# A decoder trunk in which GLA and HGRN2 make and turn their carried keys later, and score products are tied into runs

## The chip, the cores and the metric

The kernel runs on one core of one Trainium2 chip, as one program. The metric is the device time of one execution, in microseconds. The core has a matmul engine (TensorE, PE in the rows), a vector engine (VectorE, DVE), an activation engine (ScalarE, ACT), a general engine (GpSimd, POOL) and a queue engine (SyncE, SP). Each takes its own instructions strictly in the order in which they stand in its queue, and waits on semaphores for the others.

## What is computed

One layer over a sequence of 1024 tokens of width 1024. A normalised and modulated input u is multiplied by one wide matrix; four causal token mixers (RWKV-7, GLA, mLSTM, HGRN2) work on slices of the product, each result is gated, projected, merged and added to the input. GLA and HGRN2 are one recurrence, with 4 heads each:

```python
def _chunk_gla(q, k, v, log_g, chunk):
    # S_t = diag(exp(log_g_t)) S_{t-1} + k_t v_t^T,  o_t = S_t^T q_t
    def step(state, blk):
        qc, kc, vc, gc = blk
        b = jnp.cumsum(gc, axis=2)
        rel = jnp.where(causal[:, :, None], b[:, :, :, None, :] - b[:, :, None, :, :], -jnp.inf)
        attn = jnp.einsum('bhik,bhjk,bhijk->bhij', qc, kc, jnp.exp(rel))
        o = attn @ vc + jnp.einsum('bhik,bhkv->bhiv', qc * jnp.exp(b), state)
        b_last = b[:, :, -1]
        state = (state * jnp.exp(b_last)[..., None]
                 + jnp.einsum('bhjk,bhjv->bhkv', kc * jnp.exp(b_last[:, :, None] - b), vc))
        return state, o
...
p = u @ w_in[l]
y_b = _gla(gq, gk, gv, g_code, gla_gk_up[l], gla_gk_b[l], gla_norm_g[l])
y_d = _hgrn2(hq, hf, hi, lower_bounds[l], hg_norm_g[l])
```

## The kernel before

The kernel has three stages. The first makes u and runs RWKV-7. The second runs eight units in the order HGRN2 head 0, GLA pair 0, HGRN2 1, mLSTM pair 0, HGRN2 2, GLA pair 1, HGRN2 3, mLSTM pair 1 (a GLA unit is two heads on the two halves of the partitions). The third merges and projects. This text is on the second, and there on `d_quarter` (HGRN2, 16 calls) and `b_quarter` (GLA, 8 calls).

A **unit** is worked in four quarters of 256 tokens, each of two chunks of 128. Behind each quarter `units` issues a part of the next unit's projections: `project` loads a weight block of 128 columns (`wraw`, one buffer, L297), ScalarE casts it to `whi` (L303), VectorE makes the rest `wlo` (L304), and `mm3` (L314 to L316) multiplies both with u in products of 128x512, 24 for a half of the tokens. These are the long products in TensorE's queue between which all else stands. Once a unit a column of another matrix (`gw`) goes through the same single buffer `wraw` and is summed by VectorE into `gacc` (L278, L280).

A **quarter** does this. Running sums of the log decay are made over 128, 64 and 32 tokens (`cums`, L828). The values are turned (`turn`: two transposes by TensorE, L921, and a ScalarE copy out of PSUM, L926). `carried` (L831) makes the keys decayed to the chunk's end, `kt` (ScalarE L837, VectorE L840), and turns them to `kT`; the products of kT with V (L982 in HGRN2, L1125 in GLA) are what the state gains. `qe` is the query decayed from the chunk's start. The causal block of a chunk is split into seven levels of pairs of blocks of s = 64, 32, 16, 8, 4, 2, 1 tokens (`LV`). For each, `level_factor` makes the decay factors (exponents on ScalarE, for s of 16 and less a difference on VectorE before), VectorE multiplies in q and k (L975, L977; L1136, L1139), and a score product follows: 26 small ones of 64x64 a quarter in HGRN2 (L994), 14 of 128x128 in GLA (L1148, seven per chunk, and a short one for the diagonal, L1150). VectorE copies them under masks into the score matrix (`ATd` L1008, `ATb` L1156), and TensorE multiplies that with V (L1012, L1165) and qe with the state (L1013, L1161). The output is normalised and, later, turned (L889).

**The order** is made by the compiler's scheduler: on each engine the ready instruction that stands first in the program goes first, by estimated times. Two helpers bind it: `together` raises the priority of a list of products and lets all others of the list stand behind the first (`issue_after` says that what is issued in its block on that engine stands behind the given instruction). Before the change HGRN2's score products go through `together`; GLA's are issued freely, and stand where their factors come ready.

## Time and profile before

| | |
|---|---|
| median of 3 runs | 1797.45 us (1797.1 to 1800.5) |
| the profiled execution | 1800.29 us, its span 1798.1 us |
| TensorE busy | 1710.5 us, 95% of the span |
| VectorE, ScalarE, GpSimd busy | 1161.5, 753.7, 325.9 us |
| mean granted TensorE clock | 0.981 |
| share of the chain that ended last | TensorE 72%, VectorE 13%, ScalarE 5%, DMA 3% |

The profile is of one execution. A row of the timeline gives the start, the duration, the engine, the line, the operation, the tile written <- the tiles read, the form, how many records it holds, and in brackets how long the engine sat idle before it and what ended that. Matmuls are pipelined, so that the distance from one start to the next tells what one costs, not the duration. A product with a full f32 operand stands as two records, a transpose and the long products as one.

### The profile page before, as it was taken

How to read it: one execution, taken by the hardware profiler on the slowest of the kernel's cores; microseconds unless marked ns; L12 is line 12 of the kernel's file. 1: busy time of each engine (PE TensorE's matmuls, PEld its weight loads, DVE VectorE, ACT ScalarE, POOL GpSimd, SP SyncE). 2: the span in 40 equal slices, each digit the busy share in tenths (PEclk: the TensorE clock that was granted, in tenths of full speed). 3: DMA queues.
4: the chain of work that ended last, by engine and by line, in shares of the span. 5: the costliest groups of instructions: out<-in, count | busy, mean ns of one | idle time of the engine just before them, and what ended most of it. 6: DMA issues, size and time to landing. Idle time of an engine off the chain costs nothing.

```text
span 1798.1 us, 28703 instructions
## 1 busy us (share of the span) xinstructions
PE 1710.5 (95%) x10515; PEld 1363.1 (76%) x10515; DVE 1161.5 (65%) x3173; ACT 753.7 (42%) x1780; POOL 325.9 (18%) x555
## 2 busy tenths in 40 slices
PE   5989999999999999999899999999889999989998
PEld 4766777877777778787678877887668888767786
DVE  7657868668667744766777546666887653565632
ACT  5633333333343336546534463547444342222221
POOL 4621112011111120000010001000010020276410
PEclk7989999999999999999999999999999999999999
DMA  9222222222221222121121212111111135666422
GB/s 298 58 73 45 55 74 66 50 71 56 59 77 47 71 55 59 48 65 39 56 59 51 68 47 66 60 54 39 56 48 57 54 97 187 200 215 200 136 89 76
DMA packets 224278, 147.30 MB, mean 82 GB/s; under 512 B 60511, under 2 KB 203018, under 8 KB 224138
## 3 DMA queue, kind: packets, MB, share of 16 engines
q1 hardware_dynamic: 208800, 109.23, 22.3%
q10 hardware_dynamic: 15338, 36.24, 5.6%
q8 instruction: 83, 1.36, 0.3%
q14 instruction: 57, 0.47, 0.1%
HBM read 111.88 MB, written 33.56 MB: 81 GB/s over the span
## 4 chain that ended last, share of the span: by engine, by line
PE 72%; DVE 13%; ACT 5%; DMA 3%; POOL 3%; issue 3%; SPq 0%; POOLq 0%; ACTq 0%; DVEq 0%
PE pj L314 15%; PE pj L316 15%; PE pj L315 14%; PE yw L732 3%; PE sc L683 3%; DMA wraw<-in_w_in_dram 2%; PE iv L315 2%; PE iv L316 2%; PE iv L314 2%; DVE adacc L229 1%; PE sc L994 1%; DVE tm L670 1%; PE sc L1148 1%; PE sc L620 1%; PE iv L921 1%
## 5 line engine op out<-in xcount | busy, mean ns | idle before, releaser
L314 PE MATMUL pj<-uh,whi 128*128 128x512 f32 x1344 | 548.8, 408 | 4.1 <-DVE rn L534 3.7
L316 PE MATMUL pj<-uh,wlo 128*128 128x512 f32 x1344 | 541.5, 403 | 0.0
L315 PE MATMUL pj<-ul,whi 128*128 128x512 f32 x1344 | 539.4, 401 | 0.0
L314 PEld LDWEIGHTS pj<-uh,whi 128*128 128x128 f32 x1344 | 255.6, 190 | 52.8 <-issue 5.1
L316 PEld LDWEIGHTS pj<-uh,wlo 128*128 128x128 f32 x1344 | 255.1, 190 | 50.0 <-issue 2.9
L315 PEld LDWEIGHTS pj<-ul,whi 128*128 128x128 f32 x1344 | 255.5, 190 | 45.4 <-issue 1.0
L303 ACT CAST whi<-wraw 128x1024 fp32r<-128x1024 f32 x89 | 93.0, 1045 | 242.8 <-PE pj L315 193.7
L304 DVE TENSOR_TENSOR wlo<-wraw,whi 128x1024 fp32r<-128x1024 f32 (+1 forms) x88 | 107.1, 1217 | 50.5 <-ACT whi L303 45.8
L882 POOL TENSOR_SCALAR ss<-ss 128x2 f32<-128x2 f32 x48 | 13.4, 280 | 568.2 <-ACT on L881 566.6
L670 DVE TENSOR_TENSOR tm<-nb,xr 32x1 f32<-32x1 f32 (+14 forms) x240 | 71.4, 298 | 6.0 <-DMA nb<-nd 0.3
L891 DVE SCALAR_TENSOR_TENSOR y<-yw,DV,z 128x256 f32<-128x256 f32 x48 | 22.2, 479 | 63.2 <-PE yw L889 62.8
L1410 ACT ACTIVATE g<-pj 128x512 f32<-128x512 f32 x64 | 38.0, 594 | 56.2 <-PE pj L316 48.3
L672 DVE TENSOR_REDUCE xr<-tm 32x1 f32<-32x1 f32 (+14 forms) x240 | 54.1, 225 | 6.5
L314 PE MATMUL iv<-yt,whi 128*128 128x512 f32 x128 | 50.4, 397 | 6.8 <-ACT yt L1422 5.2
L1469 POOL TENSOR_TENSOR acc<-acc,g 128x512 f32<-128x512 f32 x32 | 46.7, 1475 | 50.3 <-DVE g L1467 50.3
L745 DVE SCALAR_TENSOR_TENSOR Gbd<-Gbd,fa,yw 64x64 f32<-64x64 f32 x128 | 35.8, 279 | 27.9 <-PE yw L732 25.9
L535 POOL TENSOR_TENSOR rn<-rn,nhalf 128x4 f32<-128x4 f32 x16 | 19.5, 1222 | 186.9 <-DVE rn L534 171.4
L314 PE MATMUL pj<-yt,whi 128*128 128x512 f32 x128 | 50.4, 394 | 1.8 <-DVE g L1467 1.8
L315 PE MATMUL iv<-yt,whi 128*128 128x512 f32 x128 | 50.1, 393 | 0.5 <-DVE yt L1423 0.5
L316 PE MATMUL pj<-yt,wlo 128*128 128x512 f32 x128 | 50.0, 390 | 0.6 <-DVE wlo L1435 0.6
L315 PE MATMUL pj<-yt,whi 128*128 128x512 f32 x128 | 50.0, 390 | 0.0
L316 PE MATMUL iv<-yt,wlo 128*128 128x512 f32 x128 | 49.7, 390 | 0.0
(483 smaller groups left out, 3406.8 us busy)
## 6 DMA issues: line engine op xcount, KB each, us to landing
wraw<-in_w_in_dram SPq DMA_DIRECT2D x89, 512.0 KB
gdram<-g ACTq DMA_DIRECT2D x64, 256.0 KB
th<-gdram ACTq DMA_DIRECT2D x32, 512.0 KB
adaw<-in_ada_w_dram SPq DMA_DIRECT2D x16, 512.0 KB
ydram<-y SPq DMA_DIRECT2D x64, 128.0 KB
wraw<-in_w_branch_dram SPq DMA_DIRECT2D x16, 512.0 KB
yr<-ydram SPq DMA_DIRECT2D x32, 256.0 KB
x<-in_x_dram SPq DMA_DIRECT2D x8, 512.0 KB
```

The lines of the kernel that those rows point to most:

```text
L303: nc.scalar.copy(hi[:, :nk, :width], raw[:, :nk, :width])
L304: eng.tensor_tensor(lo[:, :nk, :width], raw[:, :nk, :width], hi[:, :nk, :width].bitcast(F32), ALU.subtract)
L314: nc.tensor.matmul(ps[:width, :], lhsT=a, rhs=xh[:, k, :], start=k == 0, stop=False)
L315: nc.tensor.matmul(ps[:width, :], lhsT=a, rhs=xl[:, k, :], start=False, stop=False)
L316: nc.tensor.matmul(ps[:width, :], lhsT=b, rhs=xh[:, k, :], start=False, stop=k == nk - 1)
L670: nc.vector.tensor_tensor(t2, n2[:, 0:i, i].unsqueeze(1).broadcast_to([32, i, i]), x2[:, 0:i, 0:i].rearrange("p j l -> p l j"), ALU.mult)
L672: nc.vector.reduce_sum(x2[:, i, 0:i], t2, axis=AX.X)
L683: mm = lambda o, l, r: nc.tensor.matmul(o, lhsT=l, rhs=r, start=True, stop=True)
L732: mm = lambda o, l, r, **kw: nc.tensor.matmul(o, lhsT=l, rhs=r, skip_group_check=True, **kw)
L745: nc.vector.scalar_tensor_tensor(Gn[hr, hr], Gc[hr, hr], fa[hr, c : c + 1], yw[hr, P + 64 * h : P + 64 * h + 64], ALU.mult, ALU.add)
L1410: nc.scalar.activation(g[:], ps[:], AF.Tanh, scale=0.5)
L1469: nc.gpsimd.tensor_tensor(a, a, g[:], ALU.add)
```

## The change

In both quarters `kt` and `qe` are no longer made ahead of all levels but between the levels of s = 16 and s = 8. `carried` returns kt unturned; its turn and the products with V are issued behind the first of the score products (in GLA that of the first chunk). In GLA the seven score products of a chunk and the short one go through `together`, with the level s = 1 first. `together` returns its first instruction. The instructions are the same ones, in the same numbers, on every engine.

```diff
--- before.py
+++ after.py
@@ -838,7 +838,7 @@
         f = self.sm.tile([P, 2], F32, tag="df", bufs=4, name=self.nm("df"))
         nc.scalar.activation(f[:], c128[:, P - 1 : QT : P], AF.Exp)
         nc.vector.tensor_tensor(kt[:, :QT], kt[:, :QT], k, ALU.mult)
-        return f, self.turn(kt, "kT")
+        return f, kt
     def level_factor(self, s, cs, lg):
@@ -963,23 +963,20 @@
         c128 = self.cums(lg, 128)
         V = self.turn(v, "V")
-        f, kT = self.carried(c128, k)
         cs = {n: self.cums(lg, n) for n in (64, 32)}
-        qe = self.h("qe")
-        nc.scalar.activation(qe[:, :QT], c128[:, :QT], AF.Exp)
-        nc.vector.tensor_tensor(qe[:, :QT], qe[:, :QT], q, ALU.mult)
         Z = []
         for s in self.LV:
+            if s == 8:
+                f, kt = self.carried(c128, k)
+                qe = self.h("qe")
+                nc.scalar.activation(qe[:, :QT], c128[:, :QT], AF.Exp)
+                nc.vector.tensor_tensor(qe[:, :QT], qe[:, :QT], q, ALU.mult)
             x = self.level_factor(s, cs, lg)
             sp = lambda t: t[:, :QT].rearrange("p (b z t) -> p b z t", z=2, t=s)
             nc.vector.tensor_tensor(sp(x)[:, :, 1, :], sp(x)[:, :, 1, :], sp(q)[:, :, 1, :], ALU.mult)
             if s > 1:
                 nc.vector.tensor_tensor(sp(x)[:, :, 0, :], sp(x)[:, :, 0, :], sp(k)[:, :, 0, :], ALU.mult)
             Z.append(x)
-        ps_ = self.iv()
-        for c in range(2):
-            cs_ = slice(c * P, (c + 1) * P)
-            nc.tensor.matmul(ps_[:, cs_], lhsT=kT[:, cs_], rhs=V[:, cs_], start=True, stop=True)
         pd = self.yw()
         for c in range(2):
@@ -995,7 +992,14 @@
         todo = [(li, s, c, r) for li, s in reversed(list(enumerate(self.LV))) for c in range(2) for r in ((1, 0) if s < 64 else (0,))]
-        self.together([lambda t=t: level(*t) for t in todo])
+        first = self.together([lambda t=t: level(*t) for t in todo])
+        with self.tc.issue_after(first):
+            kT = self.turn(kt, "kT")
+            ps_ = self.iv()
+            for c in range(2):
+                cs_ = slice(c * P, (c + 1) * P)
+                nc.tensor.matmul(ps_[:, cs_], lhsT=kT[:, cs_], rhs=V[:, cs_], start=True, stop=True)
         AT = self.AT["d"][self.atn % 2]
         self.atn += 1
         nc.vector.copy_predicated(AT[:], self.ident[:].bitcast(U32).unsqueeze(1).broadcast_to([P, 2, P]),
@@ -1111,21 +1115,16 @@
         nc = self.nc
         c128 = self.cums(lg, 128)
         V = [self.turn(v[j], "V") for j in range(2)]
-        f, kT = self.carried(c128, k)
         cs = {n: self.cums(lg, n) for n in (64, 32)}
-        qe = self.h("qe")
-        nc.scalar.activation(qe[:, :QT], c128[:, :QT], AF.Exp)
-        nc.vector.tensor_tensor(qe[:, :QT], qe[:, :QT], q, ALU.mult)
         dg = self.h("dg")
         nc.gpsimd.tensor_tensor(dg[:, :QT], q, k, ALU.mult)
-        ps_ = self.iv()
-        for c in range(2):
-            for h in range(2):
-                hr = slice(64 * h, 64 * h + 64)
-                nc.tensor.matmul(ps_[hr, c * P : (c + 1) * P], lhsT=kT[:, c * P + 64 * h : c * P + 64 * h + 64],
-                                 rhs=V[h][:, c * P : (c + 1) * P], start=True, stop=True)
         Z, R = [], []
         for s in self.LV:
+            if s == 8:
+                f, kt = self.carried(c128, k)
+                qe = self.h("qe")
+                nc.scalar.activation(qe[:, :QT], c128[:, :QT], AF.Exp)
+                nc.vector.tensor_tensor(qe[:, :QT], qe[:, :QT], q, ALU.mult)
             x = self.level_factor(s, cs, lg)
             sp = lambda t: t[:, :QT].rearrange("p (b z t) -> p b z t", z=2, t=s)
             s5 = lambda t: t[:, :QT].rearrange("p (c b z t) -> p c b z t", c=2, z=2, t=s)
@@ -1143,11 +1142,27 @@
         for c in range(2):
             cc = slice(c * P, (c + 1) * P)
             sc = [self.sc() for _ in range(2)]
-            for li, s in enumerate(self.LV):
+            def level(li, s):
                 lhs = (k if s == 1 else Z[li])[:, cc]
-                nc.tensor.matmul(sc[li // 4][:, P * (li % 4) : P * (li % 4) + P], lhsT=lhs,
-                                 rhs=R[li][:, c].rearrange("p h t -> p (h t)"), start=True, stop=True)
-            nc.tensor.matmul(sc[1][:, 384:386], lhsT=dg[:, cc], rhs=self.bo2[:], start=True, stop=True)
+                return nc.tensor.matmul(sc[li // 4][:, P * (li % 4) : P * (li % 4) + P], lhsT=lhs,
+                                        rhs=R[li][:, c].rearrange("p h t -> p (h t)"), start=True, stop=True)
+            def own():
+                return nc.tensor.matmul(sc[1][:, 384:386], lhsT=dg[:, cc], rhs=self.bo2[:], start=True, stop=True)
+            first = self.together([lambda li=li, s=s: level(li, s) for li, s in reversed(list(enumerate(self.LV)))] + [own])
+            if c == 0:
+                with self.tc.issue_after(first):
+                    kT = self.turn(kt, "kT")
+                    ps_ = self.iv()
+                    for c_ in range(2):
+                        for h in range(2):
+                            hr = slice(64 * h, 64 * h + 64)
+                            nc.tensor.matmul(ps_[hr, c_ * P : (c_ + 1) * P], lhsT=kT[:, c_ * P + 64 * h : c_ * P + 64 * h + 64],
+                                             rhs=V[h][:, c_ * P : (c_ + 1) * P], start=True, stop=True)
             AT = self.AT["b"][c]
             for li, s in enumerate(self.LV):
                 o = AT[:].rearrange("p c (b z t) -> p c b z t", z=2, t=s)[:, :, :, 1, :]
@@ -1300,6 +1315,7 @@
             with self.tc.issue_after(first.ins):
                 for f in fs[1:]:
                     f()
+        return first.ins
     def units(self, names):
```

On TensorE, in the second quarter of GLA pair 0, there stood behind the turn of the values (`iv` written from v): the turn of kt, the four products of kT with V, the state product on qe, and the seven score products (`sc`), one at a time between long products ("...").

```order
L921 MATMUL iv_9198<-ident,v_1601_8514 128x128 x2
...
L921 MATMUL iv_9209<-ident,kt_9203 128x128 x2
...
L1125 MATMUL iv_9223<-V_9201,kT_9212 64x128
...
L1161 MATMUL yw_9297<-Sbd_8308,qe_9218 128x256
...
L1148 MATMUL sc_9278<-Zr_8295,lx_9228 128x128
...
L1148 MATMUL sc_9278<-Zr_8296,lx_9235 128x128
...
L1148 MATMUL sc_9278<-Zr_8297,lx_9244 128x128
...
L1148 MATMUL sc_9278<-Zr_8288,lx_9251 128x128
...
L1148 MATMUL sc_9279<-Zr_8289,lx_9258 128x128
...
L1148 MATMUL sc_9279<-Zr_8290,lx_9265 128x128
...
L1148 MATMUL sc_9279<-Zr_8291,k_8185 128x128
L1150 MATMUL sc_9279<-bo_584,dg_9221 128x2
```

With the change the state product stands alone, 45 long products lie between the turn of the values and the first score, the chunk's seven scores stand in a row with the one of s = 1 first, and the turn of kt and the products with V stand behind them.

```order
L921 MATMUL iv_9198<-ident,v_1601_8514 128x128 x2
...
L1176 MATMUL yw_9297<-Sbd_8308,qe_9238 128x256
...
L316 MATMUL pj_9381<-uh_74,wlo_9348 128x512
L1148 MATMUL sc_9269<-Zr_8291,k_8185 128x128
L1148 MATMUL sc_9269<-Zr_8290,lx_9255 128x128
L1148 MATMUL sc_9269<-Zr_8289,lx_9248 128x128
...
L1148 MATMUL sc_9268<-Zr_8295,lx_9209 128x128
L1152 MATMUL sc_9269<-bo_584,dg_9207 128x2
L921 MATMUL iv_9278<-ident,kt_9232 128x128 x2
...
L1164 MATMUL iv_9283<-V_9196,kT_9281 64x128
L1164 MATMUL iv_9283<-V_9201,kT_9281 64x128
```

So all seven scores moved down behind the projections, and the turn and the products moved behind the scores.

On ScalarE at the same place, the copies of the values out of PSUM were followed by kt, the cast of the next weights, the copy of kT, qe and then the factors (L857 to L870).

```order
L926 COPY V_9201<-iv_9198 128x256
L837 ACTIVATE kt_9203<-c_1718_9191 128x128 x2
L839 ACTIVATE df_9206<-c_1718_9191 128x2
L303 CAST whi_9594<-wraw_9591 128x1024
L926 COPY kT_9212<-iv_9209 128x256
L1117 ACTIVATE qe_9218<-c_1718_9191 128x256
L857 ACTIVATE lx_9228<-c_1727_9214 128x64 x2
L858 ACTIVATE lx_9228<-c_1727_9214 128x2x64
L863 ACTIVATE lx_9235<-c_1728_9216 128x32 x4
L864 ACTIVATE lx_9235<-c_1728_9216 128x4x32
L869 ACTIVATE lx_9244<-lx_9244 128x256
L869 ACTIVATE lx_9251<-lx_9251 128x256
```

With the change the factors of s = 64 and 32 and the difference's magnitude of s = 16 stand ahead of kt, and kt and qe ahead of the cast; the copy of kT comes further down, behind the last factor.

```order
L926 COPY V_9201<-iv_9198 128x256
L839 ACTIVATE df_9235<-c_1718_9191 128x2
L857 ACTIVATE lx_9209<-c_1723_9203 128x64 x2
L858 ACTIVATE lx_9209<-c_1723_9203 128x2x64
L863 ACTIVATE lx_9216<-c_1724_9205 128x32 x4
L864 ACTIVATE lx_9216<-c_1724_9205 128x4x32
L869 ACTIVATE lx_9225<-lx_9225 128x256
L837 ACTIVATE kt_9232<-c_1718_9191 128x128
...
L1126 ACTIVATE qe_9238<-c_1718_9191 128x256
L303 CAST whi_9594<-wraw_9591 128x1024
L329 ACTIVATE th_9377<-pj_9352 128x512
```

So the first factors moved ahead of the cast, and nothing on ScalarE stands behind a turn by TensorE any more until the factors are done.

On TensorE, in the second quarter of HGRN2 head 0, the turn of kt and the products with V (L982) stood ahead of one run of the 26 scores (L994), with 12 long products from it to the score matrix's product (L1012).

```order
L921 MATMUL iv_8036<-ident,kt_8030 128x128 x2
...
L982 MATMUL iv_8089<-V_8028,kT_8039 128x128 x2
...
L994 MATMUL sc_8095<-lx_8086,dk_7355 64x64 x2
L994 MATMUL sc_8096<-lx_8086,dk_7355 64x64 x2
L994 MATMUL sc_8095<-lx_8080 64x64 x2
...
L994 MATMUL sc_8096<-lx_8048 64x64
...
L1012 MATMUL yw_8138<-V_8028,ATd_7304 128x128
L1013 MATMUL yw_8138<-dS_7815,qe_8045 128x128
```

With the change the run is cut behind its first four scores by the turn of kt, four long products and the two products with V. In 8 of the 16 quarters it is cut so, or in a like way; in the others it stands whole, with the turn inside it or behind it.

```order
L991 MATMUL sc_8087<-lx_8081,dk_7355 64x64 x2
L991 MATMUL sc_8088<-lx_8081,dk_7355 64x64 x2
L921 MATMUL iv_8115<-ident,kt_8054 128x128 x2
...
L1002 MATMUL iv_8120<-V_8028,kT_8118 128x128 x2
L991 MATMUL sc_8087<-lx_8075 64x64 x2
...
L991 MATMUL sc_8088<-lx_8034 64x64
...
L1016 MATMUL yw_8138<-V_8028,ATd_7304 128x128
L1017 MATMUL yw_8138<-dS_7815,qe_8060 128x128
```

So the turn and the products with V moved down by some 30 long products, into and behind the scores.

## Rows read from the trace of the kernel before

**Rows 1.** Windows: us, busy us (records) of each engine, clock, DMA.

```profile
713.00:1430.00 717.00, 686.90 (x4087) 554.42 (x4085) 489.38 (x1489) 360.84 (x988) 51.41 (x103) 0.98 0.19 54
965.00:992.00 27.00, 27.00 (x176) 22.27 (x174) 20.64 (x64) 12.39 (x35) 0.89 (x2) 1.00 0.20 59
```

**Rows 2.** What TensorE waited for, 713 to 1430 us: total, times, longest.

```profile
PE iv L921 <- DVE kt L840: 8.9, 8, 1.7
PE iv L1125 <- ACT kT L926: 4.3, 2, 2.2
...
PE yw L1012 <- DVE ATd L1008: 3.3, 2, 2.2
...
PE sc L994 <- DVE lx L975: 2.0, 2, 1.1
...
PE sc L1148 <- DVE lx L1139: 0.4, 2, 0.2
```

**Rows 3.** Timeline of TensorE, GLA pair 0: scores alone and in a row.

```profile
834.83 0.40 PE L315 MATMUL pj<-ul,whi 128*128 128x512 f32 x1
835.20 0.46 PE L1148 MATMUL sc<-Zr,lx 128*128 128x128 f32 x2
835.42 0.48 PE L316 MATMUL pj<-uh,wlo 128*128 128x512 f32 x1
835.73 0.40 PE L314 MATMUL pj<-uh,whi 128*128 128x512 f32 x1
...
840.53 0.40 PE L316 MATMUL pj<-uh,wlo 128*128 128x512 f32 x1
840.76 1.06 PE L1148 MATMUL sc<-Zr,lx 128*128 128x128 f32 x8
841.58 0.47 PE L314 MATMUL pj<-uh,whi 128*128 128x512 f32 x1
...
874.84 0.39 PE L316 MATMUL pj<-uh,wlo 128*128 128x512 f32 x1
875.07 0.38 PE L1148 MATMUL sc<-Zr,lx 128*128 128x128 f32 x2
875.21 0.48 PE L314 MATMUL pj<-uh,whi 128*128 128x512 f32 x1
```

**Rows 4.** Timeline of TensorE, second quarter of GLA pair 0.

```profile
857.68 0.60 PE L921 MATMUL iv<-ident,v 128*128 128x128 f32 x4
...
862.62 0.41 PE L921 MATMUL iv<-ident,kt 128*128 128x128 f32 x2 [1.45 <-DVE kt L840]
...
865.96 1.12 PE L1125 MATMUL iv<-V,kT 128*64 128x128 f32 x8 [2.23 <-ACT kT L926]
```

**Rows 5.** Window of the time behind these two waits.

```profile
865.50:872.30 6.80, 6.34 (x23) 5.07 (x23) 6.51 (x21) 5.22 (x20) 0.00 (x0) 0.50 0.30 78
```

**Rows 6.** Timeline of ScalarE, second and third quarter of GLA pair 0.

```profile
864.59 1.04 ACT L303 CAST whi<-wraw 128x1024 fp32r<-128x1024 f32 x1 [2.48 <-DMA wraw<-in_w_in_dram]
...
891.10 0.37 ACT L926 COPY kT<-iv 128x256 f32<-128x256 f32 x1 [1.22 <-PE iv L921]
```

**Rows 7.** Timeline of VectorE, the last factor of these quarters.

```profile
873.60 0.58 DVE L1136 TENSOR_TENSOR Zr<-lx,q 64x128 f32<-64x128 f32 x2
...
899.34 0.58 DVE L1136 TENSOR_TENSOR Zr<-lx,q 64x128 f32<-64x128 f32 x2
```

**Rows 8.** Timeline of TensorE, the third quarter's last turn of values.

```profile
882.93 0.49 PE L921 MATMUL iv<-ident,v 128*128 128x128 f32 x3
```

**Rows 9.** Timeline of TensorE, a quarter of HGRN2 head 0: its run of scores.

```profile
809.06 0.39 PE L316 MATMUL pj<-uh,wlo 128*128 128x512 f32 x1
809.38 0.46 PE L994 MATMUL sc<-lx,dk 128*64 128x64 f32 x8
...
811.17 0.50 PE L314 MATMUL pj<-uh,whi 128*128 128x512 f32 x1
811.50 0.39 PE L315 MATMUL pj<-ul,whi 128*128 128x512 f32 x1
```

## The prediction

> **What bounds the kernel now.** I read the windows first. In the stretch of the units in question, 713 to 1430 us, TensorE is busy for 686.9 of 717 us [rows 1]; VectorE, at 489.4, comes next. So what counts is, one, what stands in TensorE's queue and what each piece costs there, and two, the 30 us in which that queue waits. Then the list of TensorE's waits: the turn of kt waits 8.9 us in 8 places, the products with kT 4.3 us in 2, both together 13.2 [rows 2]. Third the timeline. From start to start a long product takes 0.23 us, and a small one set between two of them more than its share: the first example of [rows 3], a score that has to wait for its factor's semaphore, lengthens the distance 834.83 to 835.42 from 0.23 to 0.59 (0.36 more), and the next one, 835.42 to 835.73, to 0.31 (0.08 more): 0.44 us. The third example, whose factor was there long before, adds 874.84 to 875.21 less 0.23, 0.14 us. Four in a row add 840.53 to 841.58 less 0.23, 0.82 us: 0.205 each.
>
> In the HGRN2 quarters TensorE is mostly full (27.00 of 27 us, VectorE 20.64 [rows 1]); in GLA it waits, and what it waits for is a chain over VectorE and ScalarE. That is read in the second quarter of GLA pair 0: 1.45 us for kt and 2.23 us for kT [rows 4]. The second of these is no work on kT: ScalarE sat 2.48 us at the cast of the next weights until their DMA landed [rows 6], and the copy of kT stood behind the cast.
>
> **Part by part.** The sum is made against the profiled execution, 1800.3 us; it lies 2.8 above the median of the runs, 1797.45, and I take the difference off the median.
>
> *GLA's scores in rows.* Of the 112 score products 43 stand alone between long products (counted in the timeline); 24 of them add 0.33 us or more as in the first example, 6 add 0.14, 13 lie between. With the 0.08 behind them the mean is 0.42 us, against 0.205 and a share of one entry, 0.02, in a row: 0.195 saved by each, 8.4 us. Four of the 43 ran at half the clock and add some 0.8 more for that; I take it off: 7.6. Five pairs and three triples bring some 0.5 more. Turns and products with V lose entries of their own in GLA and five score-matrix products get them; I take -0.4 for these. Together **-8.5**, between -5 (if singles that needn't wait are the rule: 43 x 0.09 and a little) and -11.
>
> *HGRN2's turn and products.* 16 turns lose their own entry, and in 8 quarters the run of 26 is cut in two. Entering the run costs 809.06 to 809.38 less 0.23, 0.09 us, leaving it 811.17 to 811.50 less 0.23, 0.10 [rows 9]. A cut costs both again, 8 x 0.19 = 1.5, and a turn inside a run the same in place of an entry of its own, near nothing. The lost entries, 0.08 to 0.1 each, give back 1.4. I take **0**, with 2 us to either side.
>
> *The waits that go.* With kt made between the levels and turned behind the first score, the turn is asked for when kt has long been there, and the products with kT 3 or more long products later. **-13.2** [rows 2]. One wait of HGRN2's score matrix, 2.2 us, the longest of its row [rows 2], stood in a place (first quarter of HGRN2 3) where no long product lay between the scores and it; now nine lie there, 9 x 0.23 = 2.1: **-2.2**.
>
> *The waits that come.* The first score of a chunk is now that of s = 1, and behind it on TensorE stand all scores, the turn, the products with V and every later long product. Before, singles went out as factors came and long products filled the time between. So the question at each GLA quarter is whether TensorE gets to the scores ahead of the last factor. Second quarter: the turn of the values starts at 857.68 [rows 4]; 0.6 us of turns, 45 long products of 0.23 and a state product of half a microsecond follow: 869.1. The last factor of before was done at 873.60 + 0.58 = 874.2 [rows 7]: with the chain as it was, a wait of 5.1. But ScalarE's first factors now stand ahead of the cast that waited for the DMA, so that this wait of 2.48 us is filled with work that before came behind it; I take 2.2 off: **2.9**. Third quarter: from the last turn of values at 882.93 [rows 8] 42 long products and small ones of 1.8 us lead to 894.4, against 899.34 + 0.58 = 899.9 [rows 7], a wait of 5.5; the copy of kT held ScalarE for 1.22 us there [rows 6], and kt with qe goes behind three levels, some 1 us: **3.3**. In the first and fourth quarter the factors came just as TensorE got to them (waits of 0.2 at most [rows 2]); their distance in long products is now nearly what it was in time, and I take 0.8 and 0.3. Two units: 2 x 7.3 = **+14.6**. In the HGRN2 quarter right behind each GLA unit, where VectorE is behind (the 2.0 us for lx in [rows 2]), fewer long products lie ahead of the scores: **+1.5** for both. The bounds: 0, if all factors come in time; and 2 x (2.4 + 5.1 + 5.5 + 1.1) + 4 = 32, if no chain gets shorter (2.4 and 1.1 by the same reckoning for quarters one and four).
>
> *The clock.* Behind the waits of the second quarter the granted clock was 0.50 for 6.8 us (865.5 to 872.3 [rows 5]), which is 1.2 GHz in place of 2.4; the engine had idled 1.45 and 2.23 us within 5 us before. I count no change: the new wait of 2.9 us is likely to bring such a stretch as the old ones did. A further stretch in each third quarter would cost some 2 us each.
>
> *No cost seen.* Every engine runs the same instructions. ScalarE's copy of kT for HGRN2 keeps three long products (0.7 us) for its 0.37 us, as before. The state updates on VectorE come later, behind score copies, but are needed only by the second chunk's state product.
>
> Sum: -8.5 + 0 - 13.2 - 2.2 + 14.6 + 1.5 = **-7.8**: 1792.5 for the profiled execution, **1789.6** by the median.
>
> A rule against the change: in the rows a switch from the full array to the 128x64 tiles of HGRN2's scores and back costs 0.19 us, and the change adds switches, since the full-array turn now stands inside those runs [rows 9]. The Trainium skill, TensorEngine Tiling (Array Packing), Key Properties, says that changing the tiling mode drains TensorE. The rows agree that a switch is not free, but put it far below one long product's start distance; by the rule as a full stop the sum would be that of the fifth case below.
>
> **The rivals.**
> 1. *Forecast*: waits for kt and kT turn, for the most part, into waits for the last factor; rows of scores remain as the gain. 1789.6.
> 2. *The factors come in time.* ScalarE isn't held by kT and the estimates that place the scores hold as well as they do in HGRN2. Then no new wait: -8.5 - 13.2 - 2.2 = -24, and two stretches at half clock less, 4 us: 1770 to 1774. For it: ScalarE works 360.8 of 717 us [rows 1]. Against: VectorE is what is behind in GLA, and its work is the same.
> 3. *No difference.* The new waits eat all: they total 20 to 28 us, and the time is 1794 to 1801, within 3.6 us of 1797.45.
> 4. *Slower, by the scores' wait*: the chain to the last factor keeps its length in all eight quarters (first score at the last factor, everything queued behind it): 32 us of new waits, -24 + 32 = +8, and two more stretches at half clock, +4: 1806 to 1809. It decides from 28 us of new waits on. For it: the chain is VectorE's, and only the order in it changes. Against: the cast's 2.48 us and kT's 1.22 us leave the chain.
> 5. *Slower, by switches of the array*: each of the 16 HGRN2 quarters gets up to four more, each a full stop of about a long product's recorded 0.39 us [rows 9]: 16 x 4 x 0.39 = 25 us in place of 0, and the time is 1815. Against: entry and exit as they stand cost a quarter of that.
>
> **How the numbers follow.** A measurement of this kernel can tell about 0.2%, 3.6 us, from no change. Chances: forecast, with 1780 to 1793.8 around it, 0.63; factors in time 0.08; no difference 0.17; slower by the scores' wait 0.09; by switches 0.03. So faster 0.71, same 0.17, slower 0.12. The range 1780 to 1799 leaves out most of the second case below and the last two above. Its width is that of the new waits (0 to 32) and of the rows (-5 to -11), weighed as said.
>
> **What would show it.** The wait of the turn for kt and of the products for kT should be gone from the list of waits, and a wait of the GLA scores for a factor (Zr or lx) should stand in it with 10 to 18 us, in the second and third quarters of both units above all. Rows of seven scores should add some 1.5 us where seven singles added 2 to 3. HGRN2's quarters should be as long as before. The forecast is wrong high if the scores' waits are under 8 us, and wrong low if they pass 24 us, if half-clock stretches double, or if the HGRN2 quarters get longer by 0.3 us or more each.

## The result, and the profile of the changed kernel

The change makes the kernel slower: 1810.69 us (1809.96 to 1811.33) against 1798.28 us in the same comparison, a ratio of 1.0067 (95% interval 1.0055 to 1.0079), 12 us. The forecast was 1789.6, faster; the time lies above the whole range (1780 to 1799). The profiled execution took 1811.06 us, its span 1809.1.

TensorE's window in the changed kernel, beside [rows 1], and its waits from 700 to 1500 us, beside [rows 2]:

```profile
713.00:1430.00 717.00, 671.61 (x4024) 548.25 (x4023) 484.29 (x1483) 357.75 (x978) 57.22 (x107) 0.98 0.19 53
```

```profile
PE yw L1176 <- DVE qe L1127: 13.8, 8, 4.0
PE sc L991 <- DVE lx L976: 10.8, 12, 5.2
PE pj L314 <- ACT q L907: 5.4, 2, 5.1
...
PE yw L1016 <- DVE ATd L1012: 1.1, 1, 1.1
...
PE sc L1148 <- DVE Zr L1135: 0.8, 3, 0.3
```

The waits for kt and kT are gone, as forecast, and so is the 2.2 us for ATd. In their place stand three that the forecast did not have where they are: GLA's state product (L1176) waits for qe, HGRN2's scores (L991) for their factor in 12 places, and a long product for ScalarE's copy of q, once for 5.1 us. GLA's own scores (L1148), at which I had expected the new waits, hardly wait.

Where the 12 us come from is read from landmarks: the first turn of values of each unit in both traces, less 0.227 us for each long product that stands on the other side of it.

| us against before | HGRN2 0 | GLA 0 | HGRN2 1 | mLSTM 0 | HGRN2 2 | GLA 1 | HGRN2 3 | mLSTM 1 | third stage |
|---|---|---|---|---|---|---|---|---|---|
| changed kernel | +4.9 | -2.5 | +3.2 | -0.1 | +5.8 | -1.6 | +3.8 | +0.1 | -2.7 |

By these landmarks GLA is faster, by 4 us where 7 were forecast, and HGRN2, for which I had put down a difference of next to nothing, loses 17.7 us. They tell where time is lost, not whose change loses it. By the same landmarks in the runs below, HGRN2 changed alone loses 9.1 us in HGRN2 0 and 2 and nothing in HGRN2 1 and 3 (-0.4), the two right behind GLA; GLA changed alone makes these two 3.8 us longer, with their own quarter as before. A good part of the 7.0 us that they lose here is thus GLA's.

### The profile page after: what moved, and what is told of

Read it like the earlier page. It is cut to its first block, busy times and chain, and to the rows that moved or that the text cites. A ratio compares the mean times of both kernels' runs of the same rounds, so it can differ in the third digit from the quotient of the medians.

```text
span 1809.1 us, 28615 instructions
## 1 busy us (share of the span) xinstructions
PE 1707.6 (94%) x10515; PEld 1368.4 (76%) x10515; DVE 1156.6 (64%) x3173; ACT 754.6 (42%) x1780; POOL 330.3 (18%) x555
## 4 chain that ended last, share of the span: by engine, by line
PE 65%; DVE 18%; ACT 7%; DMA 3%; POOL 3%; issue 3%; SPq 0%; POOLq 0%; DVEq 0%; ACTq 0%
PE pj L314 12%; PE pj L316 12%; PE pj L315 12%; PE yw L732 3%; PE sc L683 3%; PE sc L991 2%; DVE adacc L229 2%; DMA wraw<-in_w_in_dram 2%; PE iv L315 1%; PE iv L314 1%; PE iv L316 1%; PE sc L1148 1%; DVE c L828 1%; DVE tm L670 1%; DVE wlo L304 1%
```

## A wait of 5 us: a gate that came late

The two steepest places are the first quarters of HGRN2 0 and HGRN2 2. Both have a GLA unit behind them, and so the program has `decay` there: two products of `gcode` with `gup` for GLA's gate, into the banks `iv`, and a chain on ScalarE. `iv` has two banks, handed out in the order of the program: turned keys, products with V, gate of half 0, gate of half 1. In the kernel before, the gate's products stood at 718.21 and 722.20. TensorE's rows of the changed kernel:

```profile
726.09 0.48 PE L1093 MATMUL iv<-gcode,gup 80*128 80x512 f32 x1
...
729.50 0.47 PE L1093 MATMUL iv<-gcode,gup 80*128 80x512 f32 x1
735.03 0.80 PE L314 MATMUL pj<-uh,whi 128*128 128x512 f32 x1 [5.06 <-ACT q L907]
```

They follow the products with kT, which now follow the score row. ScalarE, first before, then after (L1091 to L1093 before, L1095 to L1097 after, are the gate):

```profile
722.41 1.24 ACT L1091 ACTIVATE ga<-iv,PT 128x512 f32<-128x512 f32 x2
723.55 1.14 ACT L1092 ACTIVATE ga<-ga 128x512 f32<-128x512 f32 x2
724.71 1.28 ACT L1093 ACT_TABLE_LOAD   x1
726.01 1.15 ACT L1093 ACTIVATE ga<-ga 128x512 f32<-128x512 f32 x2
727.07 0.57 ACT L907 COPY q<-pj 128x512 f32<-128x512 f32 x1
```

```profile
726.60 0.69 ACT L1095 ACTIVATE ga<-iv,PT 128x512 f32<-128x512 f32 x1 [3.04 <-PE iv L1093]
727.32 0.63 ACT L1096 ACTIVATE ga<-ga 128x512 f32<-128x512 f32 x1
727.97 1.28 ACT L1097 ACT_TABLE_LOAD   x1
729.27 0.63 ACT L1097 ACTIVATE ga<-ga 128x512 f32<-128x512 f32 x1
...
731.24 0.69 ACT L1095 ACTIVATE ga<-iv,PT 128x512 f32<-128x512 f32 x1
731.95 1.28 ACT L839 ACT_TABLE_LOAD   x1
733.78 0.20 ACT L839 ACTIVATE df<-c 128x2 f32<-128x2 f32 x1 [0.55 <-DVE c L828]
733.89 0.61 ACT L1096 ACTIVATE ga<-ga 128x512 f32<-128x512 f32 x1
734.41 0.56 ACT L907 COPY q<-pj 128x512 f32<-128x512 f32 x1
```

Before, both halves of the gate ran together on ScalarE with one table load, and the first copy of q came at 727.07. After, ScalarE sits idle for 3.04 us until the first product is there, the halves come 4.6 us apart, with table loads of 1.28 us among them, and the copy that frees the bank `pj` comes at 734.41. TensorE waits 5.06 us for it, and its granted clock is at half for 6.8 us from 732.4 on (window of the changed kernel, last columns the clock, DMA share and GB/s):

```profile
732.40:739.20 6.80, 4.17 (x10) 3.30 (x11) 6.80 (x11) 5.70 (x8) 4.41 (x6) 0.50 0.00 0
```

## An account by waits, clock and the rest

For every run I divide the second stage (first turn of values of HGRN2 0 to that of mLSTM pair 1's last quarter) into TensorE's idle time, half of the time at granted clock 0.50, and the rest. Half a stretch is an estimate: long products start 0.43 us apart in a stretch (735.62 to 736.05 in the changed kernel), 0.23 at full clock. Idle time inside a stretch is counted in both columns, 0.5 to 5.7 us, so that the rest is up to 2.9 us too low.

| kernel | ratio to before | second stage | waits | at half clock (stretches) | rest |
|---|---|---|---|---|---|
| before | 1 | 763.6 | 30.2 | 27.2 (5) | 719.8 |
| before, second trace | 1 | 759.9 | 29.5 | 20.4 (5) | 720.2 |
| changed | 1.0067 | 777.3 | 45.6 | 30.6 (6) | 716.4 |
| HGRN2 old in two quarters | 1.0024 | 765.5 | 38.7 | 17.0 (4) | 718.3 |
| only those two new | 1.0045 | 770.4 | 34.6 | 30.6 (6) | 720.4 |
| GLA alone | 0.9997 | 762.1 | 35.6 | 23.8 (5) | 714.6 |
| HGRN2 alone | 1.0056 | 769.2 | 36.3 | 20.4 (4) | 722.6 |
| gate first | 1.0059 | 767.9 | 43.1 | 23.8 (5) | 712.8 |
| GLA alone, qe early | 0.9955 | 753.4 | 30.4 | 13.6 (3) | 716.2 |
| GLA alone, rows only | 1.0005 | 761.7 | 36.7 | 13.6 (3) | 718.2 |
| GLA alone, keys and qe early | 1.0023 | 767.0 | 41.9 | 27.2 (4) | 711.6 |
| HGRN2 alone, turn late | 1.0028 | 765.0 | 35.6 | 20.4 (5) | 719.1 |
| HGRN2 alone, keys amid | 1.0109 | 778.9 | 38.1 | 27.2 (5) | 727.2 |
| GLA alone, state product bound | 0.9956 | 750.1 | 32.0 | 6.8 (2) | 714.6 |
| the same, qe early too | 0.9990 | 762.2 | 34.6 | 27.2 (8) | 714.0 |
| changed, qe early | 1.0008 | 761.2 | 36.9 | 13.6 (2) | 717.6 |
| HGRN2 new in 14 quarters | 1.0021 | 764.0 | 33.0 | 17.0 (4) | 722.5 |
| combination | 0.9965 | 752.8 | 33.6 | 17.0 (3) | 710.7 |

The stage is that of one execution, the ratio that of all; they differ by up to 6 us, and the ratio decides. In the gate-first run the gate's products, and 13 long products that before came behind it, stand ahead of the first landmark, which makes its stage look 3.9 us shorter than it is.

## Experiments

**Which part loses, and where.** Two runs change one unit kind alone; three others split HGRN2's quarter between the two calls with a gate behind them and the 14 others.

```diff
+    def d_quarter(self, hd, qi, *a):
+        return (self.d_quarter_old if qi == 0 and hd in (0, 2) else self.d_quarter_new)(hd, qi, *a)
```

This stands in the first and the fifth of the runs below; the second has `not (...)` around the condition, and the others take the old or the new function throughout.

> The changed kernel, with HGRN2's quarter as it was before the change in 2 of its 16 calls: the first quarters of HGRN2 0 and 2, the units behind which a GLA unit follows. Theory A (the gate of the next GLA unit): its two products share the two banks of PSUM named iv with the turned keys and the products with V; made late, these push the gate back, and ScalarE's gate work with its table loads then stands ahead of the copy that frees a bank for the long products. In the trace of the changed kernel the distance to the kernel before grows by 5.2 us in the first such quarter and its neighbour and by 4.4 us in the second. So 9.6 us come back: 1801 us (1799.5 to 1803). Theory B (every quarter of HGRN2 pays: factors late on VectorE, rows cut): 2 of 16 shares of some 17 us, 2.2 us come back: 1808.5 us. Theory C (GLA's wait for qe is the loss): nothing comes back, 1810 to 1811.

> The mirror image: the kernel before, with HGRN2's new quarter in those two calls alone. Theory A: 1798.3 + 9.6, so 1808 us (1805 to 1809), with a wait of a long product for ScalarE's copy of some 5 us in the first of the two. Theory B: 1798.3 + 2.2 = 1800.5. Theory C: 1798.3.

Measured: 1.0024 (1.0014 to 1.0034) where the changed kernel has 1.0067, so 8 of 12 us come back; and 1.0045 (1.0033 to 1.0057), 8 us, with those two quarters alone. Theory A: in the first kernel's trace HGRN2 0 is as long as before (-0.3 us) and HGRN2 2 loses 2.0 in place of 5.8. In the second kernel's trace the stall is the same one:

```profile
732.72 0.80 PE L314 MATMUL pj<-uh,whi 128*128 128x512 f32 x1 [5.07 <-ACT q L907]
```

> The change in GLA's quarter alone; HGRN2 as before. In the trace of the changed kernel the GLA units end 2.45 and 1.6 us nearer to the kernel before than they began, though TensorE waits 13.8 us for qe in them. Theory A and B both: 1798.3 - 4 = 1794 us (1791 to 1797). Theory C (the qe wait is the loss): slower than 1798.3, 1800 to 1806.

> The change in HGRN2's quarter alone; GLA as before. Theory A and B both: the four HGRN2 units lose 17 us between their first and last landmarks in the changed kernel, of which some 2.7 are given back in the third stage: 1811 to 1815 us. Theory C: 1798.

Measured: GLA alone 0.9997 (0.9988 to 1.0006), neither the gain nor the loss that I expected; HGRN2 alone 1.0056 (1.0043 to 1.0069). So HGRN2 carries the loss, and GLA, which should have carried the gain, brings none.

> HGRN2's quarter new in 14 of its 16 calls, old in the first quarters of HGRN2 0 and 2; GLA as before. Theory A (the two quarters carry the loss): the whole of HGRN2's change cost 1.0056, the two alone 1.0045: what is left is 1.000 to 1.002. Theory B (every quarter pays for cut rows and late factors): 14 of 16 shares of 10 us, 1.005.

Measured: 1.0021 (1.0010 to 1.0031), 4 us, just above theory A's end. The two quarters with a gate have two thirds of HGRN2's loss, the other 14 one third.

**The gate ahead of the quarter.**

```diff
             for q in range(4):
+                if q == 0 and n in dec:
+                    dec[n]()
                 quarter(q)
```

`dec[n]` is the `decay` of the GLA unit that follows, taken out of the step in which it stood.

> The changed kernel, both quarters new in all calls, but the gate of a GLA unit (its two products and the work on ScalarE and VectorE behind them) is issued ahead of the HGRN2 unit's first quarter in place of behind it, so that it takes the two iv banks before the turned keys do. Theory A (the gate is pushed back by the late turn and then holds ScalarE in front of the copies): the 8 us that the first experiment got back by undoing two quarters come back here with all 16 quarters new: 1.0010 to 1.0030 of the kernel before, and no wait of 5 us of a long product for the copy near 735 us. Theory B (it is HGRN2's own row of scores, its factors and its turn that are late in those two quarters): no change against the changed kernel, 1.0067.

Measured: 1.0059 (1.0045 to 1.0073), not clearly different from the changed kernel's 1.0067, so the 8 us didn't come back. The wait for the copy is gone, but in HGRN2 0 another of the same size stands 4 us earlier: the gate's work is now ahead of the quarter's factors.

```profile
731.26 0.48 PE L991 MATMUL sc<-lx,dk 128*64 128x64 f32 x4 [4.82 <-DVE lx L976]
```

HGRN2 2 loses 1.1 us there in place of 5.8. So the copy does stand behind the gate, but moving the gate was no cure. In the kernel before, the gate ran just between the factors and the copies. That the first quarter lacks room for the gate's chain beside the factors is my reading; no run shows it by itself.

**Late turn or late keys.**

Against HGRN2's new quarter, GLA old. The first makes keys and qe ahead of the levels:

```diff
+        f, kt = self.carried(c128, k)
         cs = {n: self.cums(lg, n) for n in (64, 32)}
+        qe = self.h("qe")
...
-            if s == 8:
-                f, kt = self.carried(c128, k)
-                qe = self.h("qe")
```

The second leaves them late and puts turn and products ahead of the scores in the program:

```diff
+        kT = self.turn(kt, "kT")
+        ps_ = self.iv()
...
         pd = self.yw()
...
-        with self.tc.issue_after(first):
-            kT = self.turn(kt, "kT")
-            ps_ = self.iv()
```

> HGRN2 alone: keys and qe made ahead of the levels as before the change, only the turn and the products with V issued behind the first score; GLA as before. No row of scores is cut in it: the turn stands behind the whole row of 26, and in the first quarters of HGRN2 0 and 2 the gate of the next GLA unit stands behind it again. Theory A (the late turn pushes the gate back in these two quarters): the loss of the two-quarter experiment comes back nearly whole, 1.003 to 1.005. Theory B (factors late behind keys and qe on VectorE, and cut rows): none of it here: 0.999 to 1.001.

> HGRN2 alone, the other half: keys and qe made between the levels of 16 and 8, but the turn and the products with V in the program ahead of the scores as before; GLA as before. The scheduler puts the turn late all the same, since the keys are late: 11 rows are cut, the gate stands behind the row. Theory A: as slow as with the turn alone late, 1.003 to 1.005. Theory B: as slow as HGRN2's whole change, 1.0056, where the turn alone costs nothing. If both hold, this one has 1.005 to 1.007 and the other 1.003 to 1.005.

Measured: 1.0028 (1.0017 to 1.0040), just under theory A, and 1.0109 (1.0093 to 1.0126), above all that was expected. With the turn alone late the stall of the first quarter is there (first row below), and HGRN2 0 and 2 lose 2.7 and 5.7 us, while HGRN2 1 and 3 are 2.2 and 2.4 us shorter. So it is the late turn that costs in the units with a gate behind them, without late keys and with the score row cut in none of their first quarters. With the keys late and the turn not bound behind the scores it is worse than all else. The turn waits for kt in 16 places (second row); 5 of these, 7.6 us, are GLA's own, as with HGRN2's whole change. By the account the 9.7 us that it loses against that change are 1.8 of waits, 3.4 of clock and 4.6 in the rest, with 11 rows cut.

```profile
732.56 0.80 PE L314 MATMUL pj<-uh,whi 128*128 128x512 f32 x1 [4.50 <-ACT q L907]
```

```profile
PE iv L921 <- DVE kt L840: 13.9, 16, 1.7
```

**GLA's missing gain.** Five kernels have HGRN2 as before and GLA's new quarter with an edit. The first makes qe ahead of the levels:

```diff
         cs = {n: self.cums(lg, n) for n in (64, 32)}
+        qe = self.h("qe")
+        nc.scalar.activation(qe[:, :QT], c128[:, :QT], AF.Exp)
+        nc.vector.tensor_tensor(qe[:, :QT], qe[:, :QT], q, ALU.mult)
...
                 f, kt = self.carried(c128, k)
-                qe = self.h("qe")
-                nc.scalar.activation(qe[:, :QT], c128[:, :QT], AF.Exp)
-                nc.vector.tensor_tensor(qe[:, :QT], qe[:, :QT], q, ALU.mult)
```

The second keeps of the change the rows alone; the third is the first with `carried` ahead of the levels too.

> GLA's quarter new, but qe made ahead of the levels as before the change; HGRN2 as before. With the change in GLA alone TensorE waits 13.8 us in 8 places for qe at the state product, which stands ahead of the score rows. Theory D: the wait goes and only the second quarters' scores then wait, since the last factor is done 15.45 us behind the turn of the values and TensorE would be at the scores 16.63 - 3.99 = 12.64 us behind it: 2 x 2.8, and 1 to 2 us elsewhere; so 5 to 7 us faster than with GLA changed alone, 0.9955 to 0.9975 of the kernel before. Theory E: qe ahead of the levels pushes all factors back by as much and the wait moves to the scores whole: 0.999 to 1.001.

> Of the change only the rows: GLA's seven scores and the short one tied together, s = 1 first; keys and qe made ahead of the levels and kT turned and multiplied as before the change; HGRN2 as before. By the working of the prediction: rows -8.5 us, the waits for kt and kT stay, and the scores wait for the last factor where TensorE comes early: 15 us or more by the bounds (28 less the 13 that TensorE has already waited): +6 us, 1.002 to 1.005. Rival: the scheduler sets the rows where the factors are ready, and the rows pay whole: 0.995.

> GLA's quarter new in its rows and in the late turn, but keys and qe both made ahead of the levels; HGRN2 as before. Theory D: as with qe early alone, but the keys' work on ScalarE and VectorE, some 1 us a quarter, stands ahead of the factors, and the scores wait that much longer where they wait at all: 1 to 4 us slower than with qe early alone, 0.996 to 0.999. Theory E: as slow as the kernel before, or slower: 1.000 to 1.003.

Measured: 0.9955 (0.9943 to 0.9968), 1.0005 (0.9996 to 1.0014) and 1.0023 (1.0013 to 1.0033). The rows alone lie between theory and rival: they lower the rest by 1.6 us and raise the waits by 6.5. The longest, 5.00 us (1.10 before), stands in the HGRN2 quarter right behind GLA 1, whose own code is as before. With qe made early alone GLA gains 8 us. Its waits then stand where the prediction had placed them, at the scores:

```profile
PE sc L1145 <- DVE Zr L1132: 6.1, 8, 2.4
PE yw L1173 <- DVE qe L1118: 5.0, 5, 1.6
```

By the account the second stage is 8.7 us shorter than with GLA changed alone: 5.2 of waits and 5.1 of clock (10.2 us less at half), with 1.6 more in the rest. The clock is that of one execution: over all of them its mean was 0.9852, against 0.9840 for the kernel before in the same comparison, some 2 of the 8 us. Making the keys early as well costs 12 us against that, three times the upper end of my estimate: TensorE waits 11.5 us more, 7.6 of it in two places where a product with the score matrix waits for VectorE (9.6 us, 2.0 with qe alone early).

The other two bind the state product behind the first score of its chunk, with qe late and with qe early:

```diff
             po = self.yw()
-            nc.tensor.matmul(po[:, 0:256], lhsT=qe[:, cc], rhs=S[:].rearrange("p h t -> p (h t)"), start=True, stop=False,
-                             skip_group_check=True)
+            with self.tc.issue_after(first):
+                nc.tensor.matmul(po[:, 0:256], lhsT=qe[:, cc], rhs=S[:].rearrange("p h t -> p (h t)"), start=True, stop=False,
+                                 skip_group_check=True)
```

> GLA's quarter new with qe made late as in the changed kernel, but the state product too is bound behind the first score of its chunk, so that nothing on TensorE asks for qe ahead of the scores; HGRN2 as before. Theory D (qe's wait at the state product is GLA's loss, and behind it little is late): the 13.8 us turn into 5 to 8 at the scores, as with qe made early: 0.9945 to 0.997. Theory E (it was the place of qe on ScalarE and VectorE, not the wait): the wait moves to the scores whole, 0.999 to 1.001.

> Both: qe made ahead of the levels and the state product bound behind the first score; HGRN2 as before. With qe made early alone TensorE still waits 5.0 us in 5 places for qe and 6.1 in 8 for Zr. Theory D: if the state product's wait is all that is left of qe, some 2 us more come back (the rest turns into waits for Zr): 0.9935 to 0.996. Rival: qe made early costs the factors what the wait gives back, and this is as fast as or slower than with qe late: 0.996 or more.

Measured: 0.9956 (0.9944 to 0.9969) and 0.9990 (0.9981 to 1.0000). Leaving qe late but asking for it behind the first score is worth as much as making it early. So it was the wait in TensorE's queue, not the work on VectorE. Both together should have been best and were not. The rest is the same (714.0 and 714.6). TensorE waits 2.6 us more, and its clock is at half in 8 stretches against 2. In these two traces that is 10.2 us, but over all executions the mean granted clock was 0.9832 against 0.9850, which is some 3 of the 6 us between the ratios. The first scores of GLA 0's fourth quarter in each kernel, and the window behind the first:

```profile
920.80 0.46 PE L1145 MATMUL sc<-Zr,k 128*128 128x128 f32 x2 [1.37 <-DVE Zr L1132]
```

```profile
921.90:925.30 3.40, 3.40 (x17) 3.31 (x16) 1.36 (x5) 0.37 (x1) 0.00 (x0) 0.50 0.00 0
```

```profile
922.29 0.46 PE L1145 MATMUL sc<-Zr,k 128*128 128x128 f32 x2 [1.37 <-DVE Zr L1132]
```

Behind the wait of 1.37 us in the slower kernel the clock fell for 3.4 us; behind the same wait in the other it did not.

**Do the parts add up, and what is best?** The changed kernel with the first GLA edit above; a combination of the bound state product, HGRN2's late turn and the old quarter in the two calls; the kernel before, unedited.

> The changed kernel, both quarters new, but GLA's qe made ahead of the levels. Theory: GLA's part of the loss and HGRN2's add up. With GLA changed alone this edit took the ratio from 0.9997 to 0.9955; the same 0.0042 off the changed kernel's 1.0067 gives 1.0025 (1.001 to 1.004), with half-clock stretches of GLA's second quarters gone. Rival: in the whole, HGRN2's stalls take the gain back: 1.005 or more.

Measured: 1.0008 (0.9997 to 1.0018), just under the theory's range: this one edit takes 10 us off the changed kernel. HGRN2 1 and 3, which lose 7.0 us in the changed kernel, lose nothing here (-0.7); HGRN2 0 and 2 still lose 9.1.

> What the runs so far point to: GLA new with the state product bound behind the first score; in HGRN2 keys and qe made ahead of the levels as before, the turn and its products behind the score row, but as before the change in the first quarters of HGRN2 0 and 2. Theory: the late turn pays where no gate stands behind it: in the run with the turn alone late, HGRN2 1 and 3 were 2.2 and 2.4 us shorter than before. So 4 us on top of the 0.9956 of GLA alone: 0.993 to 0.9945. Rival: those 4 us were the GLA units' overhang and not HGRN2's, and nothing is added: 0.9956 or more.

Measured: 0.9965 (0.9952 to 0.9978): the rival. The combination adds nothing; HGRN2's scores wait 9.4 us in it, 5.7 of it in HGRN2 3's first quarter. The two kernels with GLA alone, at 0.9955 and 0.9956, beat both the kernel before and the changed one.

> The kernel before, unchanged, for a second trace on the chip of these runs. If the comparison of stretches between traces holds from chip to chip, the stretch from HGRN2 0's first turn of values to mLSTM pair 1 is as long as in the first trace (763.7 us) within 1 us, with half-clock stretches in the same places, and what differs between executions lies in the first stage. Rival: the second stage itself differs by 2 us or more from chip to chip.

Measured: 759.9 us in place of 763.6, the rival. What differs most is the clock behind the two waits of each second quarter of GLA: at half for 6.8 us in the first trace [rows 5], for 3.4 in this one, where the waits for kT are a little shorter (1.80 and 1.86 us, 2.23 and 2.10 in the first):

```profile
864.50:867.90 3.40, 3.21 (x13) 2.50 (x14) 3.35 (x10) 2.17 (x10) 0.00 (x0) 0.51 0.34 91
867.90:871.30 3.40, 3.40 (x18) 2.84 (x18) 3.33 (x13) 3.25 (x10) 0.00 (x0) 0.99 0.21 63
```

## Why the prediction was wrong, step by step

*The waits that go*: right. All 15.4 us are out of the list.

*GLA's scores in rows*: right for the scores, too much for the stage. By the distances from start to start, idle time left out, the scores of both units cost 40.0 us beyond the long products before, 30.7 with GLA alone and 31.9 with the rows alone: 8 to 9 us less, as forecast (-8.5, between -5 and -11). But the rest of the second stage falls by less, by 5.2 us with GLA alone (719.8 to 714.6) and by 1.6 with the rows alone, so that something else costs more; what it is wasn't traced.

*The waits that come, GLA*: the size right (15.2 us at the state product and the scores, 14.6 forecast), the place wrong. The step that failed reads "45 long products of 0.23 and a state product of half a microsecond follow". I counted that product as time and didn't ask what it needs. It needs qe, which the change makes later, and the scheduler had put it ahead of the scores. In the second quarter:

```profile
872.96 1.19 PE L1176 MATMUL yw<-Sbd,qe 128*128 128x256 f32 x2 [3.99 <-DVE qe L1127]
...
881.17 1.06 PE L1148 MATMUL sc<-Zr,lx 128*128 128x128 f32 x8
```

The scores run eight microseconds behind it without a wait. With GLA changed alone TensorE's waits rise by 5.4 us in all (30.2 to 35.6), which takes back the 5.2 of the rest. That the same edit without this wait gives 8 us shows that the forecast for GLA, -7 us, could have been had.

*HGRN2's turn and products, 0*: mis-sized. I read quarters at full clock, with idle time left out and the longer distance behind each piece counted in. Scores, turn and products with V cost 2.71 us (median) beyond the long products before, and the same in the changed kernel where the row stays whole; they cost 3.03 where the turn or the products stand in it. That is 0.32 in each of 11 quarters, 3.5 us; HGRN2 alone has +2.8 in its rest. I had charged 0.19 for a cut, in 8 quarters, next to nothing for a turn inside a whole row, and given 1.4 back. A cut row:

```profile
757.19 0.45 PE L991 MATMUL sc<-lx,dk 128*64 128x64 f32 x8 [0.42 <-DVE lx L976]
757.57 0.44 PE L921 MATMUL iv<-ident,kt 128*128 128x128 f32 x2
757.76 0.48 PE L316 MATMUL pj<-uh,wlo 128*128 128x512 f32 x1
...
758.77 0.60 PE L1002 MATMUL iv<-V,kT 128*128 128x128 f32 x4
759.30 1.62 PE L991 MATMUL sc<-lx 128*64 128x64 f32 x44
```

*HGRN2's scores, +1.5*: too small. The first row above shows what I had not looked for: before, the scores started just as the last factor was done, with nothing to spare: in the quarter of [rows 9] it was done at 808.97 + 0.29 = 809.26, and the scores start at 809.38.

```profile
808.97 0.29 DVE L975 TENSOR_TENSOR lx<-lx,q 128x128 f32<-128x128 f32 x1
```

Now they wait in 12 places, 10.8 us in all, 2.0 before [rows 2]. Two things bring that about. With the turn alone late, so that less stands ahead of them on TensorE, they wait 6.1 us in 9 places; with keys and qe late as well it is 7.6 in 12. And one wait, 5.23 us in HGRN2 3's first quarter, is nearly half of the sum:

```profile
1354.22 0.69 PE L991 MATMUL sc<-lx,dk 128*64 128x64 f32 x8 [5.23 <-DVE lx L976]
```

It is 1.10 us before, 1.86 with HGRN2 changed alone and 3.46 with GLA changed alone. This is one of the two places for which I had put down the +1.5. The other was misread: of the 2.0 us, 0.86 stood in HGRN2 1's third quarter, not behind GLA.

*No cost seen*: the costliest step. "Every engine runs the same instructions" is true and hid the worst: the turn's banks of PSUM have a next user. Two quarters, 8 of the 12 us. It did not decide the sign alone: without them the kernel is still 4 us slower than before. My own sign of a forecast that is too low, HGRN2 quarters longer by 0.3 us or more each, came true: HGRN2 alone loses 10 us in 16.

*The clock, no change*: true of the changed kernel (27.2 us at half clock before, 30.6 after). In the better variants it is a smaller part than their single traces say: by the mean of all executions some 2 us of 8 with qe early, and nothing clear with the state product bound (0.9850 against 0.9848).

*Rivals.* The fourth, slower by the scores' wait, gave nearly the time (1806 to 1809) by a mechanism that the trace rules out: they wait for 1.4 us. The fifth, four stops of 0.39 us in each quarter of HGRN2, would be 1.56 us a quarter; the rows show 0.32, in 11 quarters.

The Trainium skill, ScalarE: Activation LUTs, What ACT_TABLE_LOAD costs, gives 1283 ns for a load and 1380 ns more for a drain. The rows agree with the first (1.28 us) and show nothing of the second: before the change the instruction ahead ends at 724.69, the load runs from 724.71, and the next one starts at 726.01.

Left open: why the third stage is shorter wherever GLA is new, by some 2 to 3 us in nearly all of these kernels (in the changed one 1.6 us of it is less waiting of TensorE; the cause wasn't traced), why the keys' place costs 12 us in GLA, what in the gate's chain the first quarter can't hold, and why equal waits bring a stretch at half clock in one kernel and none in another.

## What to carry to other kernels

When a value is made later, list every instruction that reads it and look for the one that stands first in its engine's queue: the wait goes there, whichever consumer the change had in mind, and binding that one behind the rest can be worth as much as making the value early. When a product moves, ask for the next user of its PSUM bank, and for what that one's result sets off on other engines. A wait saved in one unit can come back at the head of the next, so look at whole runs before giving a loss to a unit. A term called zero because the instructions are the same deserves a bound like any other.

## What the runs showed of the hardware

The same kernel's stretches at half clock behind waits in the same places lasted 6.8 us in one execution and 3.4 in another, which by the account alone moves the second stage by 3.4 us. A wait of 1.37 us brought a stretch of 3.4 us in one kernel and none in its neighbour. A transpose of the full array inside a row of 64-wide scores takes 0.26 us to the next start (813.86 to 814.12 in the changed kernel), not much less than its own recorded 0.33, where one in a pair takes 0.11 (716.90 to 717.01 before).
